# Turning a token tile once: the scaled parts of x made from the raw transpose, in the first stage of a retention and MLA step

## The chip, the cores and the metric

The kernel runs on one core of one Trainium2 chip. The metric is device time in microseconds of one execution; the time before is the median of three runs, 2188.82 us (2184.98 to 2189.14).

## The reference

The reference is one inference step of a hybrid decoder layer (d_model 1024) for a prompt of 1024 tokens and for 8 sequences of 4 sampled tokens (32 rows). What the change touches is the very beginning: the normalised input and the latents that are projected from it.

```python
def rmsnorm(x, w):
    xf = x.astype(jnp.float32)
    xf = xf * lax.rsqrt(jnp.mean(xf * xf, axis=-1, keepdims=True) + EPS)
    return xf.astype(x.dtype) * w

def mixer_inputs(x, pos, ln_w, w_in, q_norm_w, w_uq, kv_norm_w):
    z = rmsnorm(x, ln_w) @ w_in
    rq, rk, rv, rg, cq, ckv, kr, mg, ga, gb = jnp.split(z, ...)
    ...
    q = (rmsnorm(cq, q_norm_w) @ w_uq).reshape(b, s, MLA_HEADS, MLA_QK)
    ckv = rmsnorm(ckv, kv_norm_w)
    kr = rope(kr, pos)
```

Behind it come retention over chunks of 128 tokens, MLA attention over the prompt and, for the sampled rows, over 8192 cached tokens per sequence, two down projections merged by gates, an output projection with the residual x, a per-layer embedding term and a final norm. All of that is the same in both kernels.

## The kernel before

Every large product is made in float32 quality by three matmuls of operands split in a high and a low part (`mac`: high by high, low by high, high by low). The normalised input lives transposed in SBUF, features on partitions, as eight pairs `xn[k]` of 128 features by 1056 tokens: `xh` (high) and `xl` (low).

The first stage, about the first 100 us, makes those pairs and the latents of all nine token tiles: eight of 128 prompt tokens and one of the 32 sampled rows. The tiles go in the order 0, 1, 8, 2, 3, 4, 5, 6, 7 (8 is the sampled one). For each tile:

- `norm_tile` takes the tile of raw rows `xt`. ACT squares and sums it (L337), POOL (GpSimd) makes r, the reciprocal root of the mean (L233, L235). `turn_input` transposes the raw rows on TensorE (PE, L322, eight transposes of 128x128 in two halves), ACT copies each half out of PSUM into a buffer `turn` (L323), and SP stores it in DRAM for the residual at the end (L324). Then DVE makes `xs` = xt times r (L340), PE transposes `xs` as well (L345, eight more), ACT makes `xh` = the transpose times the norm's weight (L350), and DVE `xl`, the rest (L351).
- `latent_tile` projects the tile on the 704 latent columns: 24 matmuls of 384 columns and 24 of 320 (L266 to L268, into `ac`). ACT squares (L385), POOL makes the roots, DVE scales `la` (L387) and turns the rope part (L361 to L366). One tile later, PE transposes `la` (L396, L398), and ACT and DVE copy it out as `lt` (L400, L401).
- `turn_p` transposes the tile's per-layer embedding `pl` with two transposes (L322 too).

The transposes of all kinds share a ring of three PSUM banks (`tr`), the latents another of three (`ac`). `turn` has four buffers, the raw weight chunks `wlr` (L309, split into `wlh` by ACT or POOL and `wll` by DVE, L199) also four. In the start the eight weight chunks arrive while the first two tiles are normalised. From the seventh tile on, matmuls of the next stage (`mm`, the gates) are filled in between.

The order of each engine's instructions is set by a scheduler from the order of the code and the dependencies; the queues then run strictly in that order. The main loop calls, for the n-th tile of the order, the latents, then the late transposes of the tile before, then `norm_tile` of the tile two further on:

Of the kernel before, what the change touches and what calls it, by code (L numbers as in the profile page):

```python
# [9 lines left out]
F32 = mybir.dt.float32  # L10
# [4 lines left out]
ALU = mybir.AluOpType  # L15
# [4 lines left out]
P = 128  # L20
D = 1024
# [134 lines left out]
def run(g):  # L156
    for _ in g:
        pass
# [3 lines left out]
def decode_step(ctx: ExitStack, tc: tile.TileContext, A: dict, O: dict):  # L162
    nc = tc.nc
    pe, act, dve, pool, sp = nc.tensor, nc.scalar, nc.vector, nc.gpsimd, nc.sync
# [15 lines left out]
    def tr():  # L180
        return banks["pool"].tile([P, 512], F32, tag="tr", name="tr", bufs=3)

    def ac():
        return banks["pool"].tile([P, 512], F32, tag="ac", name="ac", bufs=3)
# [7 lines left out]
    def b32(ap):  # L192
        return ap.bitcast(F32)
# [10 lines left out]
    def C(name, i=0, w=None, rows=P):  # L204
        o, ww = at[name]
        w = ww if w is None else w
        return cst[:rows, o + i * w:o + (i + 1) * w]

    ident = C("ident")
# [11 lines left out]
    xTD = dram.tile([P, 8, NT], F32, tag="xTD", name="xTD")  # L221
# [5 lines left out]
    def small(pl, tag, w=1, bufs=4):  # L227
        return pl.tile([P, w], F32, tag=tag, name=tag, bufs=bufs)

    def rstd_of(pl, ss, n, scale, by=pool, w=1):  # L230

        v = small(pl, f"rs_v{w}", w, 4 if w == 1 else 2)
        by.tensor_scalar(v[:n], ss[:n], scale, EPS, op0=ALU.mult, op1=ALU.add)  # L233
        r = small(pl, f"rs_r{w}", w, 4 if w == 1 else 2)
        pool.tensor_tensor(out=r[:n], in0=v[:n], in1=nhalf[:n].to_broadcast([n, w]), op=ALU.pow)  # L235
        return r
# [16 lines left out]
    def load_w(src, nk):  # L253

        hi, lo = wtiles()
        src = src.rearrange("(k p) f -> p k f", p=P)
        for k in range(0, nk, 4):
            ks = slice(k, min(k + 4, nk))
            stage(src[:, ks], hi[:, ks], lo[:, ks])
        return hi, lo  # L260

    def mac(out, w, x, first, last):

        wh, wl = w
        xh, xl = x
        pe.matmul(out, wh, xh, start=first, stop=False)  # L266
        pe.matmul(out, wh, xl, start=False, stop=False)  # L267
        pe.matmul(out, wl, xh, start=False, stop=last)  # L268
# [17 lines left out]
    p1 = ph.enter_context(tc.tile_pool(name="p1", bufs=2))  # L286
# [3 lines left out]
    def rows(t):  # L290
        return P if t < 8 else NR
# [9 lines left out]
    def load_x(t):  # L301
        xt = p1.tile([P, D], F32, tag="xt", name="xt", bufs=4)
        sp.dma_start(xt[:rows(t)], x_rows(t))
        xts[t] = xt
# [6 lines left out]
        lo_of(lo, raw, hi)  # L311
        wlat.append((hi, lo))

    def turn_input(t, src, dst, nf):

        n = rows(t)
        for half in range(0, nf, 4):
            st = p1.tile([P, 4, P], F32, tag="turn", name="turn", bufs=4)
            w = min(4, nf - half)
            pt = tr()  # L320
            for i in range(w):
                pe.transpose(pt[:, i * P:i * P + n], src[:n, (half + i) * P:(half + i + 1) * P], ident[:n, :n])  # L322
            act.copy(st[:, :w, :n], pt[:, :w * P].rearrange("p (a b) -> p a b", a=w)[:, :, :n])  # L323
            sp.dma_start(dst[:, half:half + w, t * P:t * P + n], st[:, :w, :n])  # L324

    def turn_p(t):
        n = rows(t)
        pl = p1.tile([P, PLE], F32, tag="pl", name="pl", bufs=2)
        sp.dma_start(pl[:n], A["p_prompt"][0, 0, t * P:(t + 1) * P, :] if t < 8 else A["p_sample"].rearrange("l b t c -> (l b t) c"))
        turn_input(t, pl, pTD, PLE // P)  # L330

    def norm_tile(t):
        n = rows(t)
        xt = xts.pop(t)
        ss = small(p1, "ss")
        xs = p1.tile([P, D], F32, tag="xs", name="xs", bufs=2)
        act.activation(xs[:n], xt[:n], AF.Square, accum_out=ss[:n])  # L337
        r = rstd_of(p1, ss, n, 1.0 / D, dve if t == 0 else pool)
        turn_input(t, xt, xTD, D // P)
        dve.tensor_scalar(xs[:n], xt[:n], r[:n], None, op0=ALU.mult)  # L340
        for half in range(2):
            pt = tr()
            for q in range(4):
                k = half * 4 + q
                pe.transpose(pt[:, q * P:q * P + n], xs[:n, k * P:(k + 1) * P], ident[:n, :n])  # L345
            for q in range(4):
                k = half * 4 + q
                src = pt[:, q * P:q * P + n]
                hi = xn[k][0][:, t * P:t * P + n]
                act.activation(hi, src, AF.Copy, scale=lnw[:, k:k + 1])  # L350
                dve.scalar_tensor_tensor(out=xn[k][1][:, t * P:t * P + n], in0=src, scalar=lnw[:, k:k + 1],  # L351
                                         in1=b32(hi), op0=ALU.mult, op1=ALU.subtract)
# [20 lines left out]
    def latent_tile(t):  # L373
        n = rows(t)
        pq, pk = ac(), ac()
        for ps, lo, w in ((pq, 0, QL), (pk, QL, KL + ROPE)):
            for k in range(8):
                xk = tuple(v[:, t * P:t * P + n] for v in xn[k])
                wk = tuple(v[:, lo:lo + w] for v in wlat[k])
                mac(ps[:n, :w], xk, wk, k == 0, k == 7)  # L380
        la = latS if t == 8 else p1.tile([P, NLAT], F32, tag="la", name="la", bufs=2)
        cq, kv, kr = la[:n, 0:QL], la[:n, QL:QL + KL], la[:n, QL + KL:NLAT].unsqueeze(1)
        for src, dst, w, nw in ((pq[:n, :QL], cq, QL, qnw), (pk[:n, :KL], kv, KL, kvw)):
            ss = small(p1, "ss2")
            act.activation(dst, src, AF.Square, accum_out=ss[:n])  # L385
            r = rstd_of(p1, ss, n, 1.0 / w)
            dve.scalar_tensor_tensor(out=dst, in0=src, scalar=r[:n], in1=nw[:n], op0=ALU.mult, op1=ALU.mult)  # L387
        rope_nat(kr, pk[:n, KL:KL + ROPE].unsqueeze(1), t, n, p1, 1, "kro")
        if t < 8:
            sp.dma_start(O["ckv_prompt"][0, 0, t * P:(t + 1) * P, :], kv)  # L390
            sp.dma_start(O["krope_prompt"][0, 0, t * P:(t + 1) * P, :], la[:, QL + KL:])
            sp.dma_start(krD[:, t, :], la[:, QL + KL:])
            yield
            pt, pt2 = tr(), tr()
            for i in range(3):
                pe.transpose(pt[:, i * P:(i + 1) * P], la[:, i * P:(i + 1) * P], ident)  # L396
            for i in range(2):
                pe.transpose(pt2[:, i * P:(i + 1) * P], la[:, (3 + i) * P:(4 + i) * P], ident)  # L398
            lt = p1.tile([P, 5, P], F32, tag="lt", name="lt", bufs=2)
            act.copy(lt[:, 0:3, :], pt[:, :3 * P].rearrange("p (a b) -> p a b", a=3))  # L400
            dve.tensor_copy(lt[:, 3:5, :], pt2[:, :2 * P].rearrange("p (a b) -> p a b", a=2))  # L401
            sp.dma_start(latD[:, :, t * P:(t + 1) * P], lt)
        else:
            sp.dma_start(O["ckv_sample"].rearrange("l b t c -> (l b t) c"), kv)
            sp.dma_start(O["krope_sample"].rearrange("l b t c -> (l b t) c"), la[:n, QL + KL:])
# [30 lines left out]
    load_x(0)  # L436
    sp.dma_start(cst[:, :head], A["consts"][:, :head])
    sp.dma_start(lnw, A["ln_w"][0].rearrange("(f p) -> p f", p=P))
    norm_tile(0)
    order = [0, 1, 8, 2, 3, 4, 5, 6, 7]  # L440
    for k in range(8):
        load_lat(k)
# [2 lines left out]
    sp.dma_start(qnw, A["q_norm_w"][0:1, :].to_broadcast([P, QL]))  # L445
    sp.dma_start(kvw, A["kv_norm_w"][0:1, :].to_broadcast([P, KL]))
    sp.dma_start(ropeM, A["ropeM"])
    norm_tile(order[1])
    load_x(order[3])

    def latents():
        due = iter(())
        for n, t in enumerate(order):
            tile_ = latent_tile(t)
            next(tile_, None)
            run(due)
            due = tile_
            if n + 2 < 9:
                norm_tile(order[n + 2])
            if n + 4 < 9:  # L460
                load_x(order[n + 4])
            turn_p(t)
            if n == 1:
                sp.dma_start(cst[:, head:], A["consts"][:, head:at["turn"][0]])
                sp.dma_start(gnw, A["ret_gn_w"][0].rearrange("(f p) -> p f", p=P))
            if n == 4:
                page_rows()
            yield 7.1 if n > 5 else 0.0
        run(due)

    beside(latents(), 3 * 7.1, fill, 36)
    ph.close()

# [938 lines left out]
    for f in range(8):  # L1412
        w = load_w(A["w_down_mla"][0, :, f * P:(f + 1) * P], 8)
        gb = gate(gbD, f)
        M.append(xs_("M", dt=F32))
        out = M[f]
# [9 lines left out]
    for half in range(2):  # L1426
        for f in range(8):
            w = load_w(A["w_down_ret"][0, half * 1024:(half + 1) * 1024, f * P:(f + 1) * P], 8)
# [35 lines left out]
    for f in range(8):  # L1464
        fs = slice(f * P, (f + 1) * P)
        xT = nxt_xT
        w = load_w(A["w_out"][0, :, fs], 8)
# [11 lines left out]
        if f in (3, 4):  # L1479
            k = f - 3  # L1480
# [113 lines left out]
```

## Time and profile before

| | |
|---|---|
| median of three runs | 2188.82 us (2184.98 to 2189.14) |
| the profiled execution, its own time | 2187.65 us |
| its span | 2185.8 us |
| granted TensorE clock | 0.995 |
| PE busy | 2138.7 us, 98% |
| DVE, ACT, POOL busy | 1234.5, 731.1, 317.4 us |
| sample latents begin | 32.29 us |
| one steady tile of the first stage | 11.05 us (66.17 to 77.22) |

The span is the time between the first and the last instruction in the trace; the execution's own time also holds what lies around it (1.85 us here). Busy time is per engine over the whole span; in stretches of the first stage it differs, which is why the stage is looked at by itself. L-numbers are lines of the kernel before, unless they are said to be of the kernel after, in which this part stands up to nine lines lower.

### The profile page before, as it was taken

To read this page: it belongs to the slowest core of one execution; us is meant where nothing else is said; L and a number is where in the kernel's file an instruction comes from. 1 tells how busy PE (TensorE), PEld (TensorE's weight loads), DVE (VectorE), ACT (ScalarE), POOL (GpSimd) and SP (SyncE) were. 2 spreads that over 40 slices of the span, in tenths; PEclk is the share of its full clock that TensorE was granted. 3 is DMA by queue.
4 is the path that set the end of the run, shared out by engine and by line. 5 is a ranking of instruction groups with operands and counts; after the bars stand their busy time and mean duration, and the time that the engine had idled before them with its cause. 6 is when DMAs were issued, how large, how long until landed. Compare 5 with 4: busy or idle time off the path is not lost.

```text
span 2185.8 us, 38552 instructions
## 1 busy us (share of the span) xinstructions
PE 2138.7 (98%) x15368; PEld 1858.5 (85%) x15368; DVE 1234.5 (56%) x2776; ACT 731.1 (33%) x1537; POOL 317.4 (15%) x511
## 2 busy tenths in 40 slices
PE   8999999999999999999999999899998999999997
PEld 7997877777777898888788887788887999999997
DVE  5424564565655356656666664778676353444465
ACT  6412322333333222221222311454556342222243
POOL 2211111111110022222121220122221000000121
PEclk9999999999999999999999999999999999999999
DMA  8447666566565321532613517110112353234243
GB/s 239 136 139 263 213 218 230 177 250 216 211 231 178 112 68 49 172 116 88 208 41 121 179 52 252 51 37 12 38 51 73 130 197 98 82 96 124 78 143 115
DMA packets 264356, 299.71 MB, mean 137 GB/s; under 512 B 26544, under 2 KB 221744, under 8 KB 260080
## 3 DMA queue, kind: packets, MB, share of 16 engines
q1 hardware_dynamic: 254960, 213.36, 31.5%
q0 software_dynamic: 9216, 83.89, 10.2%
q8 instruction: 121, 1.98, 0.4%
q14 instruction: 59, 0.48, 0.1%
HBM read 233.03 MB, written 64.17 MB: 136 GB/s over the span
## 4 chain that ended last, share of the span: by engine, by line
PE 61%; issue 4%; DVE 3%; DMA 1%; ACT 1%; POOL 1%; POOLq 0%; ACTq 0%; DVEq 0%; SPq 0%
PE mm L266 15%; PE mm L267 14%; PE mm L268 14%; PE ac L266 2%; PE ac L268 2%; PE ac L267 2%; PE mm L1302 2%; PE tr L1288 1%; PE ac L1245 1%; PE sc L652 1%; PE tr L852 1%; PE x L683 1%; PE ac L874 1%; PE ac L1246 1%; PE ac L1247 1%
## 5 line engine op out<-in xcount | busy, mean ns | idle before, releaser
L266 PE MATMUL mm<-xh,wh 128*128 128x352 f32 x1344 | 458.3, 341 | 1.0 <-ACT gev L413 0.8
L267 PE MATMUL mm<-xl,wh 128*128 128x352 f32 x1344 | 436.5, 325 | 0.0
L268 PE MATMUL mm<-xh,wl 128*128 128x352 f32 x1344 | 435.5, 324 | 0.0
L266 PEld LDWEIGHTS mm<-xh,wh 128*128 128x128 f32 x1344 | 253.1, 188 | 104.2 <-issue 86.5
L267 PEld LDWEIGHTS mm<-xl,wh 128*128 128x128 f32 x1344 | 254.3, 189 | 5.0 <-issue 2.7
L268 PEld LDWEIGHTS mm<-xh,wl 128*128 128x128 f32 x1344 | 253.9, 189 | 1.5 <-issue 1.5
L199 DVE TENSOR_TENSOR wl<-wr,wh 128x512 fp32r<-128x512 f32 (+2 forms) x251 | 168.5, 683 | 133.2 <-ACT wh L247 107.0
L247 ACT CAST wh<-wr 128x512 fp32r<-128x512 f32 x216 | 129.7, 618 | 285.0 <-PE mm L267 219.9
L648 DVE STREAM_TRANSPOSE kt<-craw 128x512 f32<-128x512 f32 x256 | 160.6, 681 | 108.3 <-PE sc L652 73.1
L413 ACT ACTIVATE gev<-mm 128x352 f32<-128x352 f32 x120 | 55.6, 464 | 233.0 <-PE mm L268 151.5
L266 PE MATMUL mm<-mh,wh 128*128 128x352 f32 x384 | 124.4, 324 | 1.8 <-DVE M L1417 1.8
L268 PE MATMUL mm<-mh,wl 128*128 128x352 f32 x384 | 124.3, 324 | 0.0
L268 PE MATMUL mm<-gh,wl 128*128 128x352 f32 x384 | 124.3, 324 | 0.0
L266 PE MATMUL mm<-gh,wh 128*128 128x352 f32 x384 | 124.3, 324 | 0.0
L267 PE MATMUL mm<-ml,wh 128*128 128x352 f32 x384 | 124.2, 324 | 0.0
L267 PE MATMUL mm<-gl,wh 128*128 128x352 f32 x384 | 124.1, 323 | 0.0
L266 PE MATMUL mm<-wv,xh 128*128 128x512 f32 x256 | 103.0, 402 | 0.0
L267 PE MATMUL mm<-wv,xh 128*128 128x512 f32 x256 | 100.9, 394 | 0.0
L268 PE MATMUL mm<-wv,xl 128*128 128x512 f32 x256 | 100.7, 393 | 0.0
L841 ACT ACTIVATE on<-ac,gb,gs 128x512 f32<-128x512 f32 (+1 forms) x36 | 28.0, 778 | 208.5 <-DVE gb L839 208.2
L652 PE MATMUL sc<-kt,q 32*32 32x512 f32 x2560 | 91.5, 600 | 0.0
L1523 POOL TENSOR_TENSOR xr<-x1h,x1l 128x352 f32<-128x352 f32 x24 | 24.4, 1039 | 406.2 <-DVE pT L199 326.1
(384 smaller groups left out, 4563.0 us busy)
## 6 DMA issues: line engine op xcount, KB each, us to landing
wr<-in_w_in_dram SPq DMA_DIRECT2D x144, 256.0 KB, 3.0
st<-in_state_ret_dram SPq DMA_DIRECT2D x32, 512.0 KB, 4.1
out_ret_sample_dram<-st SPq DMA_DIRECT2D x32, 512.0 KB, 3.7
wr<-in_w_ple_gate_dram SPq DMA_DIRECT2D x48, 256.0 KB, 2.7
gt<-gev SPq DMA_DIRECT2D x48, 176.0 KB, 1.8
gl<-go SPq DMA_DIRECT2D x16, 528.0 KB, 7.6
gate<-ga SPq DMA_DIRECT2D x16, 528.0 KB, 3.3
g<-gt SPq DMA_DIRECT2D x32, 256.0 KB, 3.1
```

What stands on the lines that cost most here:

```text
L199: dve.tensor_tensor(out=out, in0=src, in1=b32(hi), op=ALU.subtract)
L247: hi_by[0](hi, raw)
L266: pe.matmul(out, wh, xh, start=first, stop=False)
L267: pe.matmul(out, wh, xl, start=False, stop=False)
L268: pe.matmul(out, wl, xh, start=False, stop=last)
L413: act.activation(t, ps, func)
L648: dve.transpose(kt[:, 2 * i + s].rearrange("p (n r) -> p n r", r=32), src)
L652: pe.matmul(sc[32 * v:32 * v + 32, q, :], Q["q4"][qs_, j + v // 2, 2 * (g % 2) + v % 2, :], kt[qs_, v, :], start=n == 0, stop=n == NJ // 2 ...
L683: pe.matmul(pv[32 * v:32 * v + 32, :KL], pT[:, n, 32 * v:32 * v + 32], keys[v % 2][:, 8 * (v // 2) + n, :], start=n == 0, stop=n == 7, til ...
L841: act.activation(on[:n], po, AF.Identity, bias=nb[:n], scale=s[:n])
L1302: pe.matmul(po[:, :256], v[a][w], t[:, x, 256 * a:256 * a + 256], start=j + a + part == 0, stop=False, skip_group_check=True)
L1523: pool.tensor_tensor(out=xr, in0=b32(x1[f][0][:, sl]), in1=b32(x1[f][1][:, sl]), op=ALU.add)
```

## The change

`norm_tile` is split. `turn_tile` squares the tile, makes r and transposes the raw rows, as before, and keeps the transposed `turn` buffers. `scale_tile` makes `xh` and `xl` from these buffers. Since features now lie on partitions and tokens along the row, r is needed as a row that is the same on all partitions: one plain float32 matmul of r, broadcast along its row, with the identity puts it in PSUM (`scale`). DVE multiplies the turned half by it into `y` (two products of 128x512), and `xh` and `xl` are made from `y`, in SBUF, no longer from PSUM. The product `xs` and the transposes of `xs` are gone. In the loop `turn_tile` is called ahead of a tile's latents, `scale_tile` behind them, both for the tile two further on. For tile 0 DVE copies the turned halves instead of ACT.

```diff
-    def turn_input(t, src, dst, nf):
+    def turn_input(t, src, dst, nf, by=act.copy):
...
-            act.copy(st[:, :w, :n], pt[:, :w * P].rearrange("p (a b) -> p a b", a=w)[:, :, :n])
+            by(st[:, :w, :n], pt[:, :w * P].rearrange("p (a b) -> p a b", a=w)[:, :, :n])
             sp.dma_start(dst[:, half:half + w, t * P:t * P + n], st[:, :w, :n])
+            turned.append(st)
+        return turned
...
-    def norm_tile(t):
+    def turn_tile(t):
         n = rows(t)
         xt = xts.pop(t)
...
         act.activation(xs[:n], xt[:n], AF.Square, accum_out=ss[:n])
         r = rstd_of(p1, ss, n, 1.0 / D, dve if t == 0 else pool)
-        turn_input(t, xt, xTD, D // P)
-        dve.tensor_scalar(xs[:n], xt[:n], r[:n], None, op0=ALU.mult)
-        for half in range(2):
-            pt = tr()
+        turned[t] = r, turn_input(t, xt, xTD, D // P, dve.tensor_copy if t == 0 else act.copy)
+
+    def scale_tile(t):
+        n = rows(t)
+        r, parts = turned.pop(t)
+        scale = tr()[:, :n]
+        pe.matmul(scale, r[:n].to_broadcast([n, P]), ident[:n, :n], start=True, stop=True)
+        for half, st in enumerate(parts):
+            y = p1.tile([P, 4, P], F32, tag="y", name="y", bufs=2)
+            dve.tensor_tensor(out=y[:, :, :n], in0=st[:, :, :n], in1=scale.unsqueeze(1).to_broadcast([P, 4, n]), op=ALU.mult)
             for q in range(4):
                 k = half * 4 + q
-                pe.transpose(pt[:, q * P:q * P + n], xs[:n, k * P:(k + 1) * P], ident[:n, :n])
-            for q in range(4):
-                k = half * 4 + q
-                src = pt[:, q * P:q * P + n]
+                src = y[:, q, :n]
                 hi = xn[k][0][:, t * P:t * P + n]
                 act.activation(hi, src, AF.Copy, scale=lnw[:, k:k + 1])
...
             tile_ = latent_tile(t)
+            if 0 < n < 7:
+                turn_tile(order[n + 2])
             next(tile_, None)
             run(due)
             due = tile_
-            if n + 2 < 9:
-                norm_tile(order[n + 2])
+            if n == 0:
+                turn_tile(order[2])
+            if n < 7:
+                scale_tile(order[n + 2])
```

On PE, at a steady tile (the stretch from 66.17 us), these rows stood behind the last latent matmul of a tile:

```order
L268 MATMUL ac<-wlh_239,xl_128 128x320
L396 MATMUL tr<-cst,la 128x128 x3
L398 MATMUL tr<-cst,la 128x128 x2
L322 MATMUL tr<-cst,xt 128x128 x8
L266 MATMUL ac<-wlh_193,xh_113 128x384
L267 MATMUL ac<-wll_194,xh_113 128x384
...
L266 MATMUL ac<-wlh_207,xh_117 128x384
L345 MATMUL tr<-cst,xs 128x128 x8
L322 MATMUL tr<-cst,pl 128x128 x2
L267 MATMUL ac<-wll_208,xh_117 128x384
```

and in the kernel after, at the same place (`rs_r` is r, so L350 is the scale matmul; L404 and L406 are the transposes of `la`, L323 those of `pl` and `xt`):

```order
L268 MATMUL ac<-wlh_234,xl_128 128x320
L404 MATMUL tr<-cst,la 128x128 x3
L406 MATMUL tr<-cst,la 128x128 x2
L350 MATMUL tr<-cst,rs_r_991 128x128
L266 MATMUL ac<-wlh_188,xh_113 128x384
L323 MATMUL tr<-cst,pl 128x128 x2
L323 MATMUL tr<-cst,xt 128x128 x8
L267 MATMUL ac<-wll_189,xh_113 128x384
```

The block of `xs` is gone, one scale matmul has come in, and `pl` and `xt` moved together to the head of the tile, one matmul behind the scale, with 47 matmuls behind them.

On DVE, beside the same stretch, before:

```order
L401 COPY lt<-tr 128x256
L387 SCALAR_TENSOR_TENSOR la<-ac,rs_r_928,kvw 128x256
L361 TENSOR_TENSOR kro_931<-ac,ropeM 128x32
L362 TENSOR_TENSOR kro_932<-ac,ropeM 128x32
L340 TENSOR_SCALAR xs<-xt,rs_r_958 128x1024
L363 TENSOR_TENSOR la<-kro_931,kro_932 128x32
...
L351 SCALAR_TENSOR_TENSOR xl_114<-tr,lnw,xh_113 128x128
L428 CAST own<-pt_all 128x512
L351 SCALAR_TENSOR_TENSOR xl_122<-tr,lnw,xh_121 128x128
```

and after (L353 makes `y`, L359 `xl`):

```order
L409 COPY lt<-tr 128x256
L395 SCALAR_TENSOR_TENSOR la<-ac,rs_r_921,kvw 128x256
L369 TENSOR_TENSOR kro_924<-ac,ropeM 128x32
L370 TENSOR_TENSOR kro_925<-ac,ropeM 128x32
L353 TENSOR_TENSOR y<-turn,tr 128x512
L371 TENSOR_TENSOR la<-kro_924,kro_925 128x32
L353 TENSOR_TENSOR y<-turn,tr 128x512
L372 TENSOR_TENSOR kro_924<-ac,ropeM 128x32
L373 TENSOR_TENSOR kro_925<-ac,ropeM 128x32
L359 SCALAR_TENSOR_TENSOR xl_114<-y,lnw,xh_113 128x128
```

The two products `y` stand where `xs` stood, and the eight `xl` follow in one row behind the rope parts.

On DVE at the start, before (`wll` is the low part of a weight chunk, in the order of the chunks: 194, 202, 208, 214 are the first four):

```order
L233 TENSOR_SCALAR rs_v_146<-ss 128x1
L340 TENSOR_SCALAR xs<-xt,rs_r_148 128x1024
L199 TENSOR_TENSOR wll_194<-wlr,wlh_193 128x704
L199 TENSOR_TENSOR wll_202<-wlr,wlh_201 128x704
L351 SCALAR_TENSOR_TENSOR xl_114<-tr,lnw,xh_113 128x128
L351 SCALAR_TENSOR_TENSOR xl_122<-tr,lnw,xh_121 128x128
L340 TENSOR_SCALAR xs<-xt,rs_r_253 128x1024
L351 SCALAR_TENSOR_TENSOR xl_116<-tr,lnw,xh_115 128x128
...
L199 TENSOR_TENSOR wll_208<-wlr,wlh_207 128x704
...
L199 TENSOR_TENSOR wll_214<-wlr,wlh_213 128x704
```

and after (189, 197, 203, 209 are the first four chunks):

```order
L324 COPY turn<-tr 128x512
L233 TENSOR_SCALAR rs_v_146<-ss 128x1
L324 COPY turn<-tr 128x512
L199 TENSOR_TENSOR wll_189<-wlr,wlh_188 128x704
L353 TENSOR_TENSOR y<-turn,tr 128x512 x2
L199 TENSOR_TENSOR wll_197<-wlr,wlh_196 128x704
L359 SCALAR_TENSOR_TENSOR xl_114<-y,lnw,xh_113 128x128
...
L359 SCALAR_TENSOR_TENSOR xl_128<-y,lnw,xh_127 128x128
L353 TENSOR_TENSOR y<-turn,tr 128x512
L199 TENSOR_TENSOR wll_203<-wlr,wlh_202 128x704
L199 TENSOR_TENSOR wll_209<-wlr,wlh_208 128x704
```

All eight `xl` of tile 0 and a third `y` now stand ahead of the third chunk's low part, and the copies of tile 0 ahead of the first.

More of the change, by code (lines that the diff above doesn't have):

```diff
@@ L312, in load_lat @@
         wlat.append((hi, lo))
-    def turn_input(t, src, dst, nf):
+    def turn_input(t, src, dst, nf, by=act.copy):
         n = rows(t)
+        turned = []
         for half in range(0, nf, 4):
@@ L330, in turn_p @@
         turn_input(t, pl, pTD, PLE // P)
-    def norm_tile(t):
+    turned = {}
+    def turn_tile(t):
         n = rows(t)
@@ L438, in decode_step @@
     sp.dma_start(lnw, A["ln_w"][0].rearrange("(f p) -> p f", p=P))
-    norm_tile(0)
+    turn_tile(0)
+    scale_tile(0)
     order = [0, 1, 8, 2, 3, 4, 5, 6, 7]
@@ L447, in decode_step @@
     sp.dma_start(ropeM, A["ropeM"])
-    norm_tile(order[1])
+    turn_tile(order[1])
+    scale_tile(order[1])
     load_x(order[3])
```

## The prediction

> **What bounds the kernel now.** I read the page first, then the busy time by stages, then TensorE's timeline through the tiles of the first stage, then what the other engines do beside it.
>
> ```profile
> span 2185.8 us, 38552 instructions
> PE 2138.7 (98%) x15368; PEld 1858.5 (85%) x15368; DVE 1234.5 (56%) x2776; ACT 731.1 (33%) x1537; POOL 317.4 (15%) x511
> ```
>
> TensorE (PE) is busy 98% of the span, so time goes where its queue gets shorter or waits less. The stretches below run from the end of one tile's latents to the end of the next; columns are window and length, then busy us and count of PE, PEld, DVE, ACT and POOL, granted clock, DMA share, GB/s.
>
> ```profile
> 0.00:32.29 32.29, 24.65 (x145) 21.47 (x146) 17.77 (x44) 20.00 (x50) 8.60 (x19) 1.00 0.81 236
> 32.29:43.66 11.37, 10.78 (x75) 7.90 (x73) 5.55 (x19) 6.75 (x20) 2.18 (x6) 1.00 0.85 232
> 43.66:54.90 11.24, 10.87 (x74) 10.13 (x72) 5.46 (x18) 6.15 (x18) 2.44 (x7) 1.00 0.83 254
> 54.90:66.17 11.27, 9.88 (x68) 9.56 (x66) 7.89 (x21) 4.85 (x15) 6.19 (x10) 1.00 0.65 168
> 66.17:77.22 11.05, 10.65 (x74) 10.11 (x72) 6.89 (x22) 7.29 (x20) 2.19 (x6) 1.00 0.54 157
> 77.22:88.27 11.05, 10.64 (x73) 10.11 (x71) 5.50 (x18) 5.39 (x16) 2.20 (x6) 1.00 0.42 120
> 88.27:92.75 4.48, 3.97 (x33) 3.47 (x30) 2.35 (x9) 2.39 (x6) 1.45 (x4) 1.00 0.47 141
> 10.00:20.00 10.00, 8.81 (x51) 7.15 (x51) 8.67 (x19) 7.53 (x19) 3.77 (x5) 1.00 0.87 240
> ```
>
> After 32.29 us PE fills nearly the whole stretch, and no other engine is near it. Before that it is busy 24.65 of 32.29 us, and DVE 8.67 of the 10 us from 10 to 20: the start is not PE's. One steady tile, on PE (start, us, line, count, idle before):
>
> ```profile
> 66.17 0.49 PE L396 MATMUL tr<-cst,la 128*128 128x128 f32 x3
> 66.72 1.27 PE L322 MATMUL tr<-cst,xt 128*128 128x128 f32 x8
> 67.74 0.42 PE L266 MATMUL ac<-wlh,xh 128*128 128x384 f32 x1
> 68.00 0.33 PE L267 MATMUL ac<-wll,xh 128*128 128x384 f32 x1
> 68.88 0.34 PE L266 MATMUL ac<-wlh,xh 128*128 128x384 f32 x1
> 69.60 1.06 PE L345 MATMUL tr<-cst,xs 128*128 128x128 f32 x8 [0.39 <-DVE la L363]
> 70.50 0.38 PE L322 MATMUL tr<-cst,pl 128*128 128x128 f32 x2
> ```
>
> The seventh 384-column matmul begins at 68.88 and occupies about 0.17 us (67.74 to 68.88 holds seven starts, the first 0.26 apart). So the xs block costs 70.50 - 69.05 = 1.45 us: 0.39 of waiting and 1.06 of its own. The other six, with their waits:
>
> ```profile
> 28.08 0.65 PE L345 MATMUL tr<-cst,xs 32*128 32x32 f32 x8 [0.60 <-DVE la L363]
> 36.09 1.06 PE L345 MATMUL tr<-cst,xs 128*128 128x128 f32 x8 [0.59 <-DVE xs L340]
> 47.06 1.06 PE L345 MATMUL tr<-cst,xs 128*128 128x128 f32 x8 [0.37 <-DVE latS L363]
> 59.58 1.09 PE L345 MATMUL tr<-cst,xs 128*128 128x128 f32 x8 [1.39 <-DVE xs L340]
> 80.66 1.06 PE L345 MATMUL tr<-cst,xs 128*128 128x128 f32 x8 [0.40 <-DVE la L363]
> 91.71 1.07 PE L345 MATMUL tr<-cst,xs 128*128 128x128 f32 x8 [0.50 <-DVE la L363]
> ```
>
> With 1.06 each (0.65 for the 32 rows), the six full blocks after 32.29 us take 1.65, 1.43, 2.45, 1.45, 1.46 and 1.56 us, 10.0 in all. That is the most that the removal itself can give there.
>
> **The change, part by part.** Removed: 72 xs transposes on PE and nine xs products on DVE. Added: nine plain-f32 matmuls that spread r, and 18 DVE products. Nearest rows:
>
> ```profile
> 187.08 1.03 PE L569 MATMUL tr<-qlT,sel 128*128 128x256 f32 x4
> 187.76 0.51 PE L266 MATMUL mm<-xh,wh 128*128 128x352 f32 x1
> L1031 DVE SCALAR_TENSOR_TENSOR st<-st,tr 128x512 f32<-128x512 f32 x32 | 20.4, 680 | 0.0
> L350 ACT ACTIVATE xh<-tr,lnw 128x128 fp32r<-128x128 f32 (+1 forms) x72 | 23.1, 357 | 15.6 <-PE tr L345 11.5 <-DVE xl L351 3.4
> 68.71 0.74 DVE L340 TENSOR_SCALAR xs<-xt,rs_r 128x1024 f32<-128x1024 f32 x1
> ```
>
> *Scale matmul.* Four plain-f32 matmuls of 256 columns take 187.08 to 187.76, 0.17 each; a transpose of 128 columns takes (67.74 - 66.72)/8 = 0.13. One standing alone, with its switch, lies between 0.13 and the 0.38 duration of a short block (the row at 70.50). I take 0.22. The Trainium skill, "FP8 and Floating Point Precision", TensorE Precision Notes, has true FP32 as four passes through the array: from the pitch of 0.17 us for 384 columns that is an estimate of 0.23 for 128, so the sum would move by under 0.1 us; for 256 columns it would give 0.45, and the trace has 0.17, so the row decides.
>
> *DVE.* Two y of 0.68 in place of one xs of 0.74 add 0.62 us a tile; DVE is busy 5.5 to 7.9 of 11. *ACT* makes hi from SBUF instead of PSUM; at 0.36 each, hi costs the same in the sum, as cover is ample: x parts are wanted only when the next latents end, and by my count of DVE's queue (kvw product from T+1.95 to 2.43, two y of 0.68, some 0.6 for rope, eight lo at 0.36 like hi) the last lo ends near T+7.3 of a stretch of 10 (T: its start). If that cover went (over 3 us late), PE would wait at its first latent matmul one for one.
>
> *New stalls.* xt, pl, la and scale now share three PSUM banks in a tighter row on PE: la x3, la x2, scale, one matmul, pl x2, xt x8. What frees the banks:
>
> ```profile
> 66.99 0.46 POOL L233 TENSOR_SCALAR rs_v<-ss 128x1 f32<-128x1 f32 x2 [2.00 <-ACT la L385]
> 66.80 0.47 ACT L400 COPY lt<-tr 128x384 f32<-128x384 f32 x1
> 66.92 0.42 DVE L401 COPY lt<-tr 128x256 f32<-128x256 f32 x1 [1.27 <-PE tr L398]
> 68.12 0.48 DVE L387 SCALAR_TENSOR_TENSOR la<-ac,rs_r,kvw 128x256 f32<-128x256 f32 x1 [0.78 <-POOL rs_r L235]
> 70.97 0.37 ACT L323 COPY turn<-tr 128x256 f32<-128x256 f32 x1
> ```
>
> From T: la 0.55, scale 0.22, a matmul 0.26: PE is at pl at T+1.03. pl's bank was la's, free when ACT's lt copy ends at 66.80 + 0.47 = T+1.10, with a hand-over of 0.2 (estimated) T+1.31. pl ends T+1.53; the first half of xt has DVE's lt copy (ended T+1.17) behind it and runs to T+1.98; the second needs pl's bank, whose ACT copy of 0.37 ends about T+2.13. So stalls of 0.28 and 0.15, 0.43 a tile. xt ends T+2.6; the remaining 47 matmuls take 7.65 (23 of 384 columns at 0.175, 24 of 320 at 320/384 of that). T+10.25 against T+11.05: 0.80 gained per steady tile.
>
> By stretch:
> - 0 to 32.29: nothing gained. What ends it is the last weight chunk, then la of tile 0, then POOL's rstds, and only behind them the sample scale:
>
> ```profile
> 10.44 0.89 DVE L199 TENSOR_TENSOR wll<-wlr,wlh 128x704 fp32r<-128x704 f32 x1 [1.56 <-POOL wlh L196]
> 10.49 0.89 POOL L233 TENSOR_SCALAR rs_v<-ss 128x1 f32<-128x1 f32 x1
> 11.47 0.56 POOL L235 TENSOR_TENSOR rs_r<-rs_v,cst 128x1 f32<-128x1 f32 x1
> 15.44 0.89 DVE L199 TENSOR_TENSOR wll<-wlr,wlh 128x704 fp32r<-128x704 f32 x1 [0.15 <-POOL wlh L196]
> 21.50 0.78 POOL L196 TENSOR_SCALAR wlh<-wlr 128x704 fp32r<-128x704 f32 x1 [4.26 <-DMA wlr<-in_w_in_dram]
> 26.02 1.06 POOL L235 TENSOR_TENSOR rs_r<-rs_v,cst 128x1 f32<-128x1 f32 x2
> ```
>
>  The sample scale comes at 27.1 with 32 matmuls behind it (4.9 us and switches): 32.3, as before. The first latent matmul now waits for the scale of tile 1, whose r ends at 12.03; PE has 48 matmuls (7.7 us) and eight small transposes to do until chunk 8 arrives past 22, so that is covered. The chunk's load needs the buffer freed by the product at 15.44.
> - 32.29 to 43.66: 1.65 leaves, but eight xt transposes of a later tile come in (1.02), a scale (0.22) and a wait of the second xt half for y (about 0.25): +0.15.
> - 43.66: 1.43 less 0.22 and 0.1: +1.1. 54.90: 2.45 less 0.22 and 0.5: +1.75. The next two: +0.80 each.
> - 88.27: 1.56 and the xt block of 1.02 (turned earlier) leave; scale 0.22 and stalls near 0.45 remain: +1.9.
>
> Sum 6.5 us. SP's queue: xt loads now stand behind the stores of the finished latents; the data are wanted a full stretch later, over 10 us, which hides it. `turn` tiles are held until y is made; ACT's copy two tiles on finds them free. Behind stage 1 both orders and waits agree, and PE is the bound, so I let the gain run through in full. The profiled execution took 2187.65 us, so 2181.15; the median of the three runs is 1.17 above it. I forecast 2182.0, inside the two.
>
> **Rivals.**
> - *The banks cost more.* If pl and both xt halves each wait for a copy and its hand-over (0.5 us more in five stretches) the gain is 4.0; with the scale at 0.38, 3: about 2185. For it: three banks, and ACT's copy at 66.80 stands behind its Square. Against: all these copies end within T+1.2 in the rows.
> - *GpSimd blocked.* At 10.49 POOL's tiny product takes 0.89 us beside a DVE subtraction of two SBUF operands, against 0.23 for one of the pair at 66.99. 72 lo now have two SBUF operands. If rstds behind them grew by 0.7 us and the kvw product, y and lo with them, by three times that a tile, the 3 us of cover would go and PE would lose some 0.5 us in five stretches: 2184.5. The Trainium skill, "SBUF — State Buffer", Who interferes with whom, states this contention; by that rule the row agrees. Against: in the new order the lo stand after kvw, so the rstds precede them.
> - *Slower: the start.* Ahead of the product at 15.44, DVE now has two copies, a third y and two more lo: 2.5 us more by the rows, against 1.71 of idle shown there. That product and the one before it each free a buffer for a load, whose way takes from 16.33 to 21.50, 5.2 us. If ACT's eight hi of tile 0, which stand ahead of its weight casts and wait for y, made both loads late by that much, the last chunk would come 10.4 + 2.5 us later and all behind it too, one for one: 2194.9. At 6.5 us of delay the gain is gone, at 11 the loss can be measured. Against: by count only about 1 us lies uncovered.
> - *Full gain.* No stalls at all: 6.5 + 2 = 8.5, 2180.
>
> **How the numbers follow.** 0.2% (4.4 us) is about what a measurement of this kernel can tell from no change. Forecast 0.50, full gain or more 0.15, banks 0.18, GpSimd 0.08, slower 0.09. Of the first two nearly all is faster by over 0.2%; the next two fall within it. Faster 0.64, same 0.27, slower 0.09. The range runs from 2177.5 (full gain and a low run) to 2187.5 (a gain of 1).
>
> **What would show it.** Right: no L345 rows; stretches near 10.25 us; pl and xt waiting 0.1 to 0.5 us for ACT and DVE copies; sample latents from about 32.3; everything later shifted by a constant. Wrong: PE idle at its first latent matmul of a tile, POOL products of 0.89 beside lo, the last chunk's weights past 23.3 us, or a gate stage that gives the gain back by waiting for weights.

## The result and the profile after

The changed kernel takes 2183.49 us (median of 11 runs, 2179.06 to 2185.05) against 2189.14 us before (11 runs of both). The ratio is 0.9977, 95% interval 0.9967 to 0.9987: by that ratio it is faster by 5.0 us, with an interval of 2.8 to 7.2. Forecast were 2182 us and a gain of 6.5. One execution of a later version (`turn_only`) took 3835.55 us at a granted clock of 0.82 and stands in no ratio. The page of the kernel after:

```profile
span 2182.7 us, 38458 instructions
PE 2133.5 (98%) x15314; PEld 1854.2 (85%) x15314; DVE 1236.4 (57%) x2787; ACT 729.2 (33%) x1535; POOL 315.9 (14%) x511
```

PE's busy time fell by 5.2 us and the span by 3.1 only. The first stage ends 3.2 us earlier in these two profiles (table below), which is nearly all that the span shows. The stretches answer to those of before, cut at the same places (the end of a tile's latents; the last ends at the eighth gate matmul):

```profile
0.00:34.59 34.59, 24.92 (x126) 23.25 (x127) 19.84 (x50) 19.22 (x49) 9.81 (x21) 0.95 0.78 229
34.59:45.72 11.13, 11.13 (x78) 8.17 (x76) 5.95 (x19) 7.41 (x21) 2.16 (x6) 1.00 0.67 176
45.72:57.59 11.87, 9.80 (x68) 9.47 (x66) 5.41 (x19) 6.18 (x18) 2.17 (x6) 1.00 0.94 266
57.59:66.92 9.33, 9.26 (x62) 9.02 (x61) 7.20 (x22) 6.97 (x19) 3.44 (x8) 1.00 0.74 199
66.92:77.03 10.11, 10.06 (x67) 9.52 (x66) 7.68 (x24) 5.31 (x16) 4.72 (x9) 1.00 0.76 209
77.03:87.14 10.11, 10.04 (x68) 9.54 (x66) 5.42 (x19) 5.30 (x16) 2.19 (x6) 1.00 0.56 159
87.14:89.54 2.40, 2.33 (x18) 2.10 (x16) 1.15 (x5) 1.22 (x4) 0.74 (x2) 1.00 0.00 0
```

| stretch | before | after | gained | forecast |
|---|---|---|---|---|
| to the sample latents | 32.29 | 34.59 | -2.30 | 0 |
| sample latents | 11.37 | 11.13 | 0.24 | 0.15 |
| the next | 11.24 | 11.87 | -0.63 | 1.1 |
| the next | 11.27 | 9.33 | 1.94 | 1.75 |
| two steady tiles | 11.05 each | 10.11 each | 1.88 | 1.6 |
| to the eighth gate matmul | 4.48 | 2.40 | 2.08 | 1.9 |
| sum | 92.75 | 89.54 | 3.21 | 6.5 |

Four of the six groups came as worked out, each a little better. Two missed, and the waits of PE name them:

```profile
PE tr L323 <- ACT xh L358: 2.1, 1, 2.1
PE tr L350 <- POOL rs_r L235: 1.9, 1, 1.9
```

The second is the spread of r for the sampled tile (the scale matmul). PE's timeline around it shows more than a wait:

```profile
25.45 0.34 PE L266 MATMUL ac<-wlh,xh 128*128 128x384 f32 x1
27.69 0.40 PE L350 MATMUL tr<-cst,rs_r 32*128 32x32 f32 x2 [1.89 <-POOL rs_r L235]
31.21 0.47 PE L266 MATMUL ac<-wlh,xh 128*128 128x320 f32 x1
31.48 0.47 PE L267 MATMUL ac<-wll,xh 128*128 128x320 f32 x1
33.27 0.31 PE L266 MATMUL ac<-wlh,xh 128*128 128x320 f32 x1
33.42 0.31 PE L267 MATMUL ac<-wll,xh 128*128 128x320 f32 x1
```

A matmul of 320 columns takes 0.27 us from start to start at 31 us and 0.15 at 33. The clock column of that stretch gives the reason:

```profile
29.40:32.80 3.40, 3.40 (x14) 3.40 (x13) 1.15 (x6) 3.12 (x10) 1.16 (x4) 0.50 0.65 186
```

For 3.4 us PE ran at half its clock, from 1.7 us behind the end of a wait of 1.9 us; 14 matmuls stand in these 3.4 us, where a second profile of this kernel (below) has 25. The first wait, of 2.1 us, is at the sampled tile's `pl`. The table names ACT. SP's queue, with the time of each issue, names another:

```profile
43.29 1.87 SPq L325 DMA_DIRECT2D xTD<-turn  x2
45.85 0.75 SPq L332 DMA_DIRECT2D pl<-in_p_sample_dram  x1
```

```profile
51.17 0.28 PE L323 MATMUL tr<-cst,pl 32*128 32x32 f32 x2 [2.07 <-ACT xh L358]
```

The load is issued at 45.85, behind stores of a tile turned ahead (`xTD`) that wait for their copies; PE has to have the data at 49.1. In the kernel before, the same load left earlier, with PE at 48.06:

```profile
41.07 0.38 SPq L329 DMA_DIRECT2D pl<-in_p_sample_dram  x1
```

### The profile page after: what moved, and what is told of

Its sections match the earlier page's. It is cut to its first block, busy times and chain, and to the rows that moved or that the text cites. A ratio compares the mean times of both kernels' runs of the same rounds, so it can differ in the third digit from the quotient of the medians.

```text
span 2182.7 us, 38458 instructions
## 1 busy us (share of the span) xinstructions
PE 2133.5 (98%) x15314; PEld 1854.2 (85%) x15314; DVE 1236.4 (57%) x2787; ACT 729.2 (33%) x1535; POOL 315.9 (14%) x511
## 4 chain that ended last, share of the span: by engine, by line
PE 61%; issue 4%; DVE 2%; ACT 1%; DMA 1%; POOL 1%; POOLq 0%; ACTq 0%; SPq 0%; DVEq 0%
PE mm L266 15%; PE mm L267 14%; PE mm L268 14%; PE ac L266 2%; PE ac L268 2%; PE ac L267 2%; PE mm L1316 2%; PE tr L1302 1%; PE sc L666 1%; PE tr L866 1%; PE ac L1259 1%; PE x L697 1%; PE ac L888 1%; PE ac L1260 1%; PE ac L1261 1%
```

## The experiments

Each ratio below is to the kernel before on the same chip. "The mark" in the text is the start of the eighth gate matmul; the expectations measure at the transposes of `la` ahead of the gates, which start 2.4 us earlier in the changed kernel (87.14 for 89.54) and 4.5 us earlier in the kernel before.

**The same kernel twice more**, for the spread between executions.

> The changed kernel once more, for a second profile. Theory A (the start is late because the sample scale waits 1.9 us for POOL's r, which stands behind the roots of tile 0's latents, and the idle PE then loses half its clock): the wait of 1.9 us and a granted clock of 0.5 for 3 to 3.5 us show again, sample latents from 34.6 us, the stretch behind them 11.1, the next 11.9 with a wait of 2.1 at the sampled tile's pl. Theory B (the half clock is an accident of that execution): clock 1.00 there and sample latents from about 33.1. Time 2183 to 2185 in both.

Measured: 2183.76 us, ratio 0.9981 (0.9972 to 0.9990). The wait is there again, the half clock is not:

```profile
27.49 0.40 PE L350 MATMUL tr<-cst,rs_r 32*128 32x32 f32 x2 [1.91 <-POOL rs_r L235]
29.40:32.80 3.40, 3.40 (x25) 3.40 (x24) 0.95 (x5) 3.13 (x9) 1.36 (x4) 1.00 0.67 217
48.96 0.28 PE L323 MATMUL tr<-cst,pl 32*128 32x32 f32 x2 [1.59 <-DMA pl<-in_p_sample_dram]
```

Sample latents began at 32.85 us and the eighth gate matmul at 87.33, 5.42 us earlier than before. So theory A was wrong that the half clock comes with the wait each time; and the start's own loss is 0.56 us, the rest of the 2.30 came mostly with the half clock. The wait at `pl` is put down to its DMA here.

> The changed kernel once more, on the same chip as the version beside it, and a third profile. Theory H: waits of 1.9 us at the sample scale and of 1.6 to 2.1 at the sampled pl; if the half clock follows one of them, the mark lies near 87, if it follows none, near 85; ratio to before 0.9975 to 0.999.

Measured: 2179.55 us on another chip, ratio 0.9972 (0.9963 to 0.9982). The scale waited 1.91 us and the clock stayed; `pl` waited 1.71, and there it fell:

```profile
50.39 0.28 PE L323 MATMUL tr<-cst,pl 32*128 32x32 f32 x2 [1.71 <-ACT xh L358]
51.50:54.90 3.40, 3.40 (x14) 3.40 (x14) 0.07 (x1) 2.08 (x4) 0.00 (x0) 0.56 0.91 262
```

The mark is at 90.34 (87.93 at the transposes of `la`, nearer to the 87 expected with one slow stretch than to 85). Between 87.33 and 90.34 one kernel's first stage differs by 3 us from profile to profile, the last of them on another chip.

**The sampled tile's r earlier.**

```diff
-            if 0 < n < 7:
+            if n < 7:
                 turn_tile(order[n + 2])
...
-            if n == 0:
-                turn_tile(order[2])
```

> The sampled tile is squared and its r made ahead of tile 0's latents. Theory A: PE does not wait for the sample scale, the clock stays 1.00, sample latents from about 31.2 us (34.59 less 1.89 of waiting and 1.5 of half clock), the rest of the stage as in the changed kernel, the time 3.4 us lower, about 2180. Theory B (half clock not from the wait): sample latents from 32.7, time 1.9 us lower. Rival C (the weights, not the wait, set the start): sample latents still past 34, time unchanged.

Measured: 2183.66 us, ratio 0.9975 (0.9965 to 0.9986), the same as the changed kernel and not the 2180 of theory A. The wait at the scale went and the sample latents began at 32.00, earlier than in any profile of the changed kernel, though not at 31.2. But PE only reached the late load sooner, and the clock fell there instead (mark 90.31):

```profile
21.96 0.40 PE L350 MATMUL tr<-cst,rs_r 32*128 32x32 f32 x2
50.44 0.28 PE L323 MATMUL tr<-cst,pl 32*128 32x32 f32 x2 [2.12 <-DMA pl<-in_p_sample_dram]
50.50:54.00 3.50, 3.50 (x19) 3.46 (x20) 0.70 (x3) 2.42 (x6) 0.00 (x0) 0.69 0.81 260
```

**pl loaded two tiles ahead.**

```diff
-    def turn_p(t):
+    def load_p(t):
...
-        pl = p1.tile([P, PLE], F32, tag="pl", name="pl", bufs=2)
+        pls[t] = pl = p1.tile([P, PLE], F32, tag="pl", name="pl", bufs=3)
...
+            if n + 2 < 9:
+                load_p(order[n + 2])
             turn_p(t)
```

> Every tile's pl is loaded two tiles ahead (three buffers in place of two); nothing else. Theory D (PE waits 2.07 us at 51.17 for the load of the sampled tile's pl, which SP issues behind stores): the wait goes, that stretch takes 9.8 us in place of 11.87, the time is 2.1 us lower, about 2181.4. Rival E (it waits for ACT or a PSUM bank, as the wait table names ACT): the stretch stays above 11.5 and the time unchanged. The start stays at 34.6 in both.

Measured: 2181.81 us, ratio 0.9964 (0.9951 to 0.9977), an interval that overlaps that of the changed kernel. Theory D holds: the stretch takes 9.91 us in place of 11.87, and nothing waits at the sampled `pl`. What ACT did at 51 us had no part in it (rival E). A new wait took its place two tiles on. In the start the wait at the scale, which this edit leaves, was 1.91 us, and the half clock followed it here too, from 29.0 to 32.4 us. The mark is at 89.54, as in the first profile of the changed kernel:

```profile
45.12:55.03 9.91, 9.88 (x67) 9.57 (x65) 5.33 (x19) 6.17 (x18) 2.18 (x6) 1.00 0.91 222
66.86 0.44 PE L323 MATMUL tr<-cst,pl 128*128 128x128 f32 x2 [1.38 <-ACT lt L412]
```

**Both together.**

> r first and pl early together, the version meant to beat both. Theories A and D: sample latents from 31.2, next stretches 11.1, 9.8, 9.3, 10.1, 10.1; the stage 5.5 us shorter than in the changed kernel, 8.7 shorter than before, time about 2178, ratio to before 0.995. If either is wrong only the other's part of it (3.4 or 2.1) shows.

Measured: 2181.46 us, ratio 0.9966 (0.9953 to 0.9979), mark 87.02, clock 1.00 through the stage. The stage is 5.7 us shorter than before where 8.7 were expected, and 2178 us were not reached. The new wait is there too, in two pieces of 0.82 and 1.09 us. ACT's timeline explains it:

```profile
61.22 1.06 ACT L346 ACTIVATE xs<-xt 128x1024 f32<-128x1024 f32 x1 [1.49 <-DVE own L440]
62.40 1.06 ACT L346 ACTIVATE xs<-xt 128x1024 f32<-128x1024 f32 x1
63.82 0.47 ACT L412 COPY lt<-tr 128x384 f32<-128x384 f32 x1
```

Two Squares write into the ring `xs`, in which `page_rows` holds the page table. They wait for its cast (L440), and the `lt` copy that frees `pl`'s bank stands behind them. The same order stands in the trace with `pl` alone.

**page_rows two tiles later** (`if n == 6` for `if n == 4`), on top of both.

> Both edits and page_rows two tiles later. In the run with both edits two Squares (L346) stood on ACT behind page_rows' cast, since they share its buffers, and the lt copy behind them: PE waited 0.82 and 1.09 us at 64 to 67. Theory F (that is all that is new there): the stretch from 62.4 falls from 12.1 to 10.1 us, the transposes of la before the gates (84.62 there, 87.14 and 84.92 in the two profiles of the changed kernel, 88.27 before) start at 82.6, no wait over 1.4 us after 13 us, clock 1.00 throughout the stage, time about 2179.5 and 0.996 of before. Rival (SP's late loads hold the tile rate): another wait appears and the mark stays at 84 or later.

Measured: 2173.19 us on a chip where the kernel before takes 2179.35, ratio 0.9972 (0.9960 to 0.9984). Theory F failed and the rival held: the Squares were free, but now DVE waited for the page table's load ahead of its own `lt` copy, PE waited 2.10 us and lost half its clock (mark 88.25):

```profile
64.66 0.43 DVE L440 CAST own<-pt_all 128x512 f32<-128x512 int32 x1 [1.53 <-DMA pt_all<-in_page_table_dram]
66.79 0.92 PE L323 MATMUL tr<-cst,xt 128*128 128x128 f32 x4 [2.10 <-DVE lt L413]
67.00:70.00 3.00, 3.00 (x12) 3.00 (x11) 3.00 (x12) 2.54 (x9) 0.62 (x1) 0.51 0.59 178
```

**The page table in the ring of xt**, loaded at the old place, used two tiles later, on top of both edits.

```diff
-        pt_all = p1.tile([P, NB * NPG], I32, tag="xs", name="pt_all", bufs=2)
+        pt_all = p1.tile([P, NB * NPG], I32, tag="xt", name="pt_all", bufs=4)
...
```

> Both edits, with page_rows' two tiles in the ring of xt (free by then) instead of the ring that the Squares write, and its load at the same place of the loop as before but its arithmetic two tiles later. In the earlier version DVE waited 1.53 us for the page table's load, ahead of the lt copy, and PE 2.10 us for that copy. Theory F2 (the page table was all that was left): no wait of PE over 1 us between 13 and 87 us, clock 1.00 there, la's transposes before the gates at 82.0 to 82.8 us, the time about 2 to 3 us under the changed kernel on the same chip. Rival: the wait moves once more (another late load), the mark at 84 or later, and the time level with the changed kernel.

Measured: 2177.80 us against 2185.39 before and 2179.55 for the changed kernel on the same chip; ratio to before 0.9960 (0.9946 to 0.9974). The mark is at 86.55, the earliest of all, 0.8 us ahead of the best profile of the changed kernel. All of PE's waits that the table groups from 13 to 90 us:

```profile
PE tr L323 <- DVE lt L413: 1.1, 1, 1.1
PE tr L323 <- DVE la L375: 0.6, 1, 0.6
PE tr L323 <- DMA xt<-in_x_prompt_dram: 0.3, 1, 0.3
```

It beats the kernel before; against the changed kernel its median is 1.75 us lower, and the intervals overlap, so that is not shown by the times. Theory F2 came half true: the clock is 1.00 through the stage, but a wait of 1.1 us is left where under 1 was expected, and the transposes of `la` start at 84.14, behind its 82.0 to 82.8 and just past the 84 of its rival.

**The two halves of the change alone.** In the first the raw rows are turned and scaled both behind the latents (`turn_tile` called just ahead of `scale_tile`), in the second they are turned ahead, but `xs` and its transposes are kept.

> The scaled parts from the raw transpose as in the changed kernel, but turned and scaled both behind the latents, at the place of before. Theory G (the gain is the xs transposes; turning ahead only removes waits): per steady tile PE has the same work as in the changed kernel and waits some 0.5 to 1 us more at the scale and the banks, 10.6 to 11.1 us a tile; time between 2183.5 and 2188. Rival (turning ahead is what pays): stretches of 11.5 or more, slower than before.

Measured: ratio 0.9987 (0.9978 to 0.9995), mark 92.43, 0.3 us earlier than before. Steady tiles took 11.3 and 10.75 us, the first of them above what theory G allowed. The transposes of `xs` are gone, and PE waits for r at the scale instead, seven times:

```profile
PE tr L350 <- POOL rs_r L235: 8.0, 7, 1.9
69.60 0.49 PE L350 MATMUL tr<-cst,rs_r 128*128 128x128 f32 x2 [1.26 <-POOL rs_r L235]
```

> Raw x turned two tiles ahead as in the changed kernel, but the scaled parts made as before (DVE's xs, eight more transposes, hi and lo from PSUM). Theory G: the transposes of xs stay, so a steady tile stays at 10.9 to 11.3 us and the time within 2186 to 2191, no gain. Rival: the order alone brings 3 us or more.

Measured: ratio 1.0004 (0.9995 to 1.0013), mark 95.17, no gain. A steady tile takes 11.0 us (81.17 to 92.17), and the `lt` copy holds up `pl` once; the clock falls to half behind that wait, from 71.8 to 75.2 us, so the mark holds this loss too:

```profile
70.49 0.44 PE L323 MATMUL tr<-cst,pl 128*128 128x128 f32 x2 [1.87 <-DVE lt L411]
```

So neither half gives the 5 us. Taking the transposes away empties PE's queue, and turning ahead is what lets PE use the room, since r is long there when the scale comes. Theory G was right on the second half; on the first its time came, at the weak end of what it allowed, and its tile rate only in one of the two steady tiles.

**A longer wait.**

> The changed kernel with six more small POOL products (about 2.8 us) in the chain of the sampled tile's r, so that PE waits about 4.5 us there instead of 1.9. Theory H (the half clock comes from idle PE, by chance of its place at 2 us, always at 4): granted clock 0.5 for about 3.4 us behind the wait, sample latents near 37. Rival (no link with the wait): clock 1.00, sample latents near 35.5.

Measured: 2180.71 us in a single execution. The wait became 4.43 us, and the clock was at half from 29.0 to 35.8 us, from within the wait on, twice the length that theory H gave; sample latents at 37.47, where it had them:

```profile
30.07 0.63 PE L360 MATMUL tr<-cst,late 32*128 32x32 f32 x2 [4.43 <-POOL late L352]
29.00:35.60 6.60, 5.54 (x20) 5.47 (x21) 2.42 (x14) 4.36 (x14) 2.19 (x7) 0.50 0.48 151
```

## Why the prediction was right, and where it was not

*Removal and steady tiles: right.* No xs transposes are left. A steady tile takes 10.11 us against T+10.25. One from 66.92, to be read beside the steady tile of before:

```profile
66.92 0.49 PE L404 MATMUL tr<-cst,la 128*128 128x128 f32 x3
67.47 0.39 PE L350 MATMUL tr<-cst,rs_r 128*128 128x128 f32 x2
67.61 0.42 PE L266 MATMUL ac<-wlh,xh 128*128 128x384 f32 x1
68.08 0.44 PE L323 MATMUL tr<-cst,pl 128*128 128x128 f32 x2
68.37 1.26 PE L323 MATMUL tr<-cst,xt 128*128 128x128 f32 x8
69.39 0.42 PE L267 MATMUL ac<-wll,xh 128*128 128x384 f32 x1
```

The scale took 67.61 - 67.47 = 0.14 us (two instructions) where 0.22 was taken. `pl` began at T+1.16 (forecast 1.31), the next matmul at T+2.47 (2.6). Both stalls are there. ACT's `lt` copy ended at T+1.11, as forecast, and `pl` began 0.05 us behind it: the hand-over of 0.2 was set too high, and that is the 0.15 us by which the tile is ahead of the forecast. The shorter scale only made PE wait longer there. The remaining 47 matmuls took 7.64 us, as forecast, though the pitches given for them add up to 7.53; the first one's 0.26 makes up most of the rest. The Trainium skill's four passes ("FP8 and Floating Point Precision", TensorE Precision Notes) would give the 0.23 estimated in the prediction; this row does not agree. The prediction's comparison with it misread a row: like the scale, each matmul of L569 stands as two instructions in the trace, so the four rows are two matmuls of 256 columns, 0.34 us each and not 0.17.

*The start: wrong.* "0 to 32.29: nothing gained" put the sample scale at 27.1, when r is there, with nothing lost ahead of it. PE was there at 25.8, since with its transposes gone it had only the last chunk's matmuls left, and the r behind tile 0's latents came at 27.6. The latents wait for the last chunk's low part, which ended at 23.67 in place of 23.20. The rival of the slow start had a delay there, but by DVE's extra work, ACT's first `xh` and a late load of the chunk. The rows show another way:

```profile
20.03 0.51 ACT L324 COPY turn<-tr 128x128 f32<-128x128 f32 x2 [2.59 <-PE tr L323]
20.74 0.77 ACT L310 CAST wlh<-wlr 128x704 fp32r<-128x704 f32 x1
21.54 1.06 DVE L199 TENSOR_TENSOR wll<-wlr,wlh 128x704 fp32r<-128x704 f32 x1 [0.32 <-ACT wlh L310]
```

ACT waited 2.59 us for PE's transposes of the sampled tile, and the cast of the seventh chunk behind them came at 20.74 (18.80 before). DVE stood idle for it, and the eighth chunk's low part came behind, though that chunk's high part was ready earlier than before (21.87 against 22.28). PE was slow ahead of these transposes: 384-column matmuls start 0.32 us apart until 15.8 us, near half rate, while in the kernel before they start 0.18 apart from 10.4 on:

```profile
14.54 0.52 PE L266 MATMUL ac<-wlh,xh 128*128 128x384 f32 x1
14.86 0.52 PE L267 MATMUL ac<-wll,xh 128*128 128x384 f32 x1
```

No run separates the slow clock at the start from the new order, so which of them cost the 0.5 us stays open. The loss was 0.56 us with the full clock behind the wait and 2.30 with half of it.

*SP's queue: wrong.* The step asked of the moved queue only whether xt comes in time. The load of `pl`, wanted in the very next stretch, moved too and was not counted. It cost 1.59 to 2.07 us in the three profiles.

*The rivals.* Banks: the two stalls take some 0.4 us in the steady tile, as in the sum, no more. GpSimd: no wait of PE behind the start leads to a POOL product of that kind. The full gain of 8.5 would have needed neither of the two misses and no stalls either.

With the full clock the sum was 5.42 of the 6.5 (the second profile), with half of it at one place 3.21 or 2.41 (92.75 less 89.54 or 90.34). The measured 5.0, interval 2.8 to 7.2, holds all but the last. That the time came so close is partly luck: in the first profile the two misses took 4.0 us from the sum and the other groups gave back 0.7, and how much the half clock takes changes from execution to execution.

## What to carry to other kernels

When work is taken from the bounding engine, list every queue whose order the change moves, and ask of each load in it, not only of the one that the change is about, when it is issued and when it is wanted. What an engine saves before a fixed arrival only becomes a wait there: two waits repaired one by one showed the next one each time, and even with both mended the stage ended only 0.3 us ahead of the best profile of the changed kernel (87.02 against 87.33), with the third 0.8 us. And a wait of TensorE near 2 us is not to be priced at its length alone.

## What the runs showed of the hardware

TensorE's clock fell to half behind some waits. Of the eleven waits of 1.5 to 2.2 us after the first 24 us, in all profiles together, six were followed by a stretch of 3.4 us at 0.50, which began 0.3 to 1.7 us behind the end of the wait; five were not; of five between 1.38 and 1.49 us none was; behind the one of 4.43 us it lasted 6.8 us. Profiles with no wait above 1.4 us there (before, both edits, the last version) had none. At half clock a 320-column matmul takes 0.27 us in place of 0.15, so a stretch of 3.4 us costs about 1.5 us on top of the wait. The Trainium skill, "TensorE: Matmul & The Clock Gate", Part 1, has the array at half rate after an idle window of about 3.4 us; the length of the stretches (3.4, and 6.8 behind the long wait) agrees, while idle of 1.7 to 2.1 us was enough at times.

Which waits are followed by it can be read from the traces. Within one trace the slow stretches begin whole multiples of 3.413 us apart (in the first profile of the changed kernel at 29.41 and 1681.46 us, 484 times that), so the time of each trace can be cut into such windows. The two waits of that profile, of 1.89 and 2.07 us, then read:

```profile
26.00:29.41 3.41, 1.72 (x10) 1.68 (x11) 2.58 (x13) 0.96 (x5) 1.42 (x4) 1.00 0.34 59
46.48:49.89 3.41, 2.63 (x16) 2.31 (x14) 2.67 (x10) 1.28 (x5) 1.43 (x4) 1.00 0.95 292
49.89:53.31 3.42, 2.14 (x16) 2.13 (x17) 2.10 (x9) 2.88 (x10) 0.00 (x0) 1.00 0.87 225
```

The first wait lies nearly whole in one window, PE is busy for 1.72 us of it, and the next window is the slow one. The second, longer wait is split between two windows, with PE busy 2.63 and 2.14 us, and none follows. All eleven cases divide so: ahead of the six slow stretches PE was busy for 1.32 to 1.72 us of the window, and in every window of the other five waits for 1.82 or more. From these figures the limit lies near half a window. One window does not fit: behind the long wait the window from 28.99, slow itself and with PE busy for 2.33 us, was followed by a second slow one. Where the windows lie differs from execution to execution, and no run here shows what sets it; that is how the same wait can cost 1.5 us more in one execution than in the next.

The clock column shows no loss ahead of the first change that a trace records. In the start of the changed kernel it reads 1.00 from 12.5 to 15.5 us, where 384-column matmuls start 0.32 us apart in place of 0.18, so the spacing is to be read there. Slow stretches stand later in the traces too, at 746 and 1415 us in the kernel before (10.2 us together) and at 1681 us in the changed one (3.4 us), so the spans of two single profiles cannot show how much of the gain ran through.
